# Feature-major projections of a two-layer sequence model: three 256-column products a step become one of 512 and one of 256

## The chip, the cores and the metric

One NeuronCore of a Trainium2 chip. The metric is device time in microseconds of one execution of the whole program, as the median of several runs. Five engines run side by side with their own instruction queues: TensorE (PE, with its weight loads shown as PEld), VectorE (DVE), ScalarE (ACT), GpSimd (POOL) and SyncE (SP, which issues most DMAs).

## The reference, cut to what matters

The model has 256 tokens, 1024 features and two layers. All data is float32.

```python
# layer 0
h = rms_norm(x, norm_w)
u = h @ w_in                      # 1024 -> 5408 columns
z_a, xbc, dt_raw, q_b, k_b, v_b, gate_lr, g_b = split_cols(u, EVEN_SPLITS)
xbc = silu(causal_depthwise_conv(xbc, conv_w, conv_b))
y_a = ssd_chunked_scan(xs, dt, a, bm, cm, d)        # state-space half
y_a = rms_norm(y_a * silu(z_a), ssd_norm_w)
o_b = gla_chunked(q_b, k_b, v_b, log_decay)         # gated linear attention half
o_b = rms_norm(o_b, gla_norm_w) * silu(g_b)
x = x + concatenate([y_a, o_b]) @ w_out
# layer 1
h = rms_norm(x, norm_w)
q, k, v, z = split_cols(h @ w_in, (1024, 1024, 1024, 1024))
o = moba_attention(q, k, v)       # 16 heads; here plain causal attention: one block of 256
x = x + (o * silu(z)) @ w_out
out = rms_norm(x, final_norm)
```

## The kernel before, in words

**Products in three parts.** Every large product is made from float32 operands cut in two: `hi`, the value rounded to the format that TensorE takes at its fast rate (float32r), and `lo`, the remainder. A product is then hi·hi + hi·lo + lo·hi, three matmuls that accumulate in one PSUM tile (`mm3`, lines 165 to 169). The contraction of 1024 is eight steps (`kb`) of 128 rows.

**Weights.** They come in pieces of up to 512 KB through the SyncE queue (`fetch`, line 70) and are split by `split` (line 75): ScalarE rounds `hi` (line 78), VectorE subtracts to get `lo` (line 79). Seven pieces are held split at a time (`NW`), and `need` (line 96) asks for a few pieces ahead of the one in use.

**Two forms of product.** In the *token-major* form (`gemm_tm`, `gemm_tt`, `part`) 128 tokens of activations are loaded as weights and 416 or 512 columns of the weight matrix stream past them. In the *feature-major* form (`gemm_fm`, line 290) 128 columns of the weight matrix are loaded and the 256 tokens of activations stream past, so the result has features on partitions. Feature-major are 26 blocks of the first projection (`pb`: blocks 0 to 9 are convolved, 10 to 13 are q and 14 to 17 k of the linear attention, 18 to 25 the gate z of the state-space half) and 24 of the attention layer's (`pp`: for each of 8 pairs of heads a q, a k and a z block). Each is 8 steps of 3 matmuls of 256 columns into the left half of a PSUM tile of 512; four such tiles rotate (`psg`).

**Evacuation.** A convolved block is scaled from PSUM into a padded buffer (`co_conv`, line 394), then four taps, a tanh and a product follow on ScalarE and VectorE. q and k blocks are copied from PSUM by ScalarE (line 578). A gate block is read from PSUM by VectorE (`gate_block`, line 591), then goes through tanh, products with `y` and a square for the norm (lines 593 to 601). In the attention layer q is copied in two halves by ScalarE (lines 748 and 749), of which only the second half is split in `hi` and `lo`; k is scaled by VectorE and split (752 to 754); z is scaled and gated (761 to 763).

**Order.** TensorE's order is fixed by the program. The projections are the main stream; the mixers (state-space pairs `co_pair`, linear attention `co_gla_pair`, attention `co_attn`) are generators whose steps are put between the projections' steps. Each `mm` adds its estimated TensorE time to a clock (`spend`, line 159), and a generator names the time that must pass before its next step (the table `DL`, line 28): `pair0` is the delay from a convolved block to its transposes, `cb` to the state-space score matrices, `gqk` before the linear attention's operands, `gla2` before the transposes `obt` of the linear attention's outputs `ob` (line 541), `at0` from a key block to the scores `as`, `at2` to the transposes `ptp` of the probabilities, `at3` to their product `ao` with the values. The other engines' queues are ordered by the compiler's scheduler, by data dependence, free buffers and the place in the program.

```python
def mm(out, lhsT, rhs, start=True, stop=True):
    ...
    TE.matmul(out, lhsT, rhs, start=start, stop=stop)
    spend(max(m / 1.2, n / 2.4) if lhsT.dtype == F32R else 2 * max(m / 1.2, n / 1.2))
```

Of the kernel before, what the change touches and what calls it, by code (L numbers as in the profile page):

```python
# [15 lines left out]
P = 128  # L16
# [6 lines left out]
NWARM = 20  # L23
# first weight pieces: (first row block, number of them)
CUTS_A0 = tuple((k, 1) for k in range(8))
AHEAD = 4
# tensor-engine time (ns) left to the other engines between the steps of a mixer
DL = {"ss": 1350, "rb": 5000, "gt": 1500, "ac": 7300, "act": 2600, "lg": 2150, "ln": 2250, "cb": 12400,
      "pair0": 11900, "pair1": 9700, "gla0": 650, "glagap": 3650, "gla1": 3350, "gla2": 8700, "r2": 10000,
      "turn": 4150, "rb1": 4000, "at0": 2600, "at2": 4350, "at3": 1800, "gqk": 250}  # L30
# feature-major blocks of the first projection: 0-9 convolved, 10-13 q, 14-17 k, 18-25 gate
# a1-a4: chunks of the token-major columns
ORDER_A = (8, 9, "a1", 0, 10, 1, 11, 2, 14, 3, 13, 5, 12, 4, 15, 16, 6, "a3", 7, 17, "a2", "a4")
GLA_NEEDS = ("a3", "a3", "a4", "a4")

# columns of the packed constants
C_EN, C_SN, C_ON = 0, 8, 16
C_CW, C_CB, C_GB, C_DS, C_GN = 24, 64, 74, 78, 86
C_DTB, C_AL = 87, 103
C_N = 119  # L40
# columns of the packed matrices of shape
M_ID, M_TRI, M_MASK, M_SEL = 0, 128, 384, 768
# [4 lines left out]
def trunk(ctx, tc, xT_d, x_d, cst_d, mat_d, gw2_d, fn_d, wa_d, wb_d, wc_d, wv_d, wp_d, wf_d, out_d):  # L47
# [20 lines left out]

    # ------------------------------------------------------------------ weights
    def fetch(src, kbs, cols, name):  # L70
# [53 lines left out]

    # ------------------------------------------------------------------ order of the tensor engine
    # The projections are the main stream; the mixers are generators that run beside it.
    # A generator yields the tensor-engine time (ns) after which its next step may be queued.
    clock = {"now": 0.0, "seq": 0}
# [16 lines left out]
    def due():  # L145
        while waiting and waiting[0][0] <= clock["now"]:
            step()
# [22 lines left out]

    # keep the tensor engine's clock up until the first operands arrive
    warm = cpool.tile([P, T], F32R, name="warm")
    V.memset(warm.bitcast(F32), 0.0)
# [3 lines left out]

    # ------------------------------------------------------------------ inputs
    xT = big.tile([P, KB, T], F32, name="xT", tag="xT")
    cst = cpool.tile([P, C_N], F32, name="cst")  # L180
    mat = cpool.tile([P, M_N], F32, name="mat")
    gw2 = cpool.tile([16, 512], F32, name="gw2")
    nc.scalar.dma_start(cst, cst_d)
# [19 lines left out]

    hhi = big.tile([P, KB, T], F32R, name="hhi", tag="hhi")
    hlo = big.tile([P, KB, T], F32R, name="hlo", tag="hlo")
    xsq = big.tile([P, KB, T], F32, name="xsq", tag="y")
# [43 lines left out]

    # ------------------------------------------------------------------ even in-projection
    v = big.tile([P, 2, D], F32, name="v", tag="v")
# [21 lines left out]
    def gemm_tm(name, hi8, lo8, cols, outs, cuts=((0, 2), (2, 2), (4, 2), (6, 2))):  # L274
        """Token-major product of both token tiles, a weight piece at a time."""
        for q_, (k0, n_) in enumerate(cuts):
            hi, lo = need((name, k0 if name == "a0" else q_))
            for tt in range(2):
                for j in range(n_):
                    kb = k0 + j  # L280
                    mm3(outs[tt][:, 0:cols], hi8[:, kb, tt * P:tt * P + P], lo8[:, kb, tt * P:tt * P + P],
                        hi[:, j, :], lo[:, j, :], kb == 0, kb == KB - 1)
# [6 lines left out]

    def gemm_fm(key, hi8, lo8, name):  # L290
        hi, lo = need(key)
        ps = pg(name)
        for kb in range(KB):
            mm3(ps[:, 0:T], hi[:, kb, :], lo[:, kb, :], hi8[:, kb, :], lo8[:, kb, :], kb == 0, kb == KB - 1)
        return ps[:, 0:T]

    def gemm_b(blk):
        return gemm_fm(("b", blk), hhi, hlo, f"pb{blk}")

# [17 lines left out]
    def co_first(ps):  # L317
# [11 lines left out]
        env["rb"] = True  # L329
        # softplus of the step sizes, by the series of artanh  # L330
        V.scalar_tensor_tensor(na, dtr, -1.0, dtr, op0=ALU.mult, op1=ALU.min)
# [29 lines left out]
        V.tensor_copy(acs, act[:, 0:32].rearrange("p (a b) -> p a b", a=2))  # L361
        # gate logits -> cumulated log decay (times 16)
        for b2 in range(2):
# [16 lines left out]

    # convolution and silu
    xs = big.tile([P, KB, T], F32, name="xs", tag="xT")
# [7 lines left out]
    def co_conv(blk, ps):  # L390
        while "rb" not in env:
            yield 100
        pd = pads[blk % 2]
        V.tensor_tensor(pd[:, 4:4 + T], ps, rb, op=ALU.mult)
        u = tmp.tile([P, T], F32, name=f"cu{blk}", tag="t1a")
        w = lambda i: cwh[:, 4 * blk + i:4 * blk + i + 1]
        S.activation(u, pd[:, 4:4 + T], AF.Identity, scale=w(3), bias=cwh[:, 40 + blk:41 + blk])
        for i in range(3):
            V.scalar_tensor_tensor(u, pd[:, 1 + i:1 + i + T], w(i), u, op0=ALU.mult, op1=ALU.add)
        th = tmp.tile([P, T], F32, name=f"cth{blk}", tag="t1b")  # L400
        S.activation(th, u, AF.Tanh)
        dst = xs[:, blk, :] if blk < 8 else bc[:, blk - 8, :]
        V.scalar_tensor_tensor(dst, th, 1.0, u, op0=ALU.add, op1=ALU.mult)
        if blk < 8:
            spawn(co_pair(blk))
        elif blk == 9:
            spawn(co_cb())
# [47 lines left out]

    # gated linear attention
    q = big.tile([P, 4, T], F32, name="q", tag="obhi")
# [108 lines left out]
    for blk in ORDER_A:  # L566
# [7 lines left out]
        if blk < 10:  # L574
            spawn(co_conv(blk, ps))
            due()
        else:
            S.activation((q if blk < 14 else k)[:, (blk - 10) % 4, :], ps, AF.Copy)
            env["nqk"] = env.get("nqk", 0) + 1
            if env["nqk"] == 8:  # L580
                spawn(co_gla_qk())

    # ------------------------------------------------------------------ gate of the state-space half
    x1 = big.tile([P, 2, D], F32, name="x1", tag="xT")
# [4 lines left out]
    def gate_block(b, ps):  # L589
        u = tmp.tile([P, T], F32, name=f"zu{b}", tag="t1a")  # L590
        V.scalar_tensor_tensor(u, ps, 0.5, rb, op0=ALU.mult, op1=ALU.mult)
        th = tmp.tile([P, T], F32, name=f"zth{b}", tag="t1b")
# [27 lines left out]

    # ------------------------------------------------------------------ even out-projection
    for n in range(2):
# [12 lines left out]
    def gemm_tt(name, hi8, lo8, tag):  # L635
        """Token-major product, one token tile after the other: yields each when it is done."""
        for tt in range(2):
            ps = pg(f"{tag}{tt}")
            part(ps, name, hi8, lo8, tt, range(KB), (name, 0) if tt == 0 else None)
            yield tt, ps  # L640

    ssn = sm.tile([P, 2, 2], F32, name="ssn", tag="ssn", bufs=1)
    h1hi = big.tile([P, KB, T], F32R, name="h1hi", tag="hhi")
    h1lo = big.tile([P, KB, T], F32R, name="h1lo", tag="hlo")

# [36 lines left out]

    # ------------------------------------------------------------------ second layer
    va = big.tile([P, 2, D], F32, name="va", tag="y")
# [54 lines left out]
    for pr in range(8):  # L739
        qk = []  # L740
        for i in range(2):
            ps = gemm_fm(("p", 3 * pr + i), h1hi, h1lo, f"pp{pr}_{i}")
            t_ = tmp.tile([P, T], F32, name=f"qk{pr}_{i}", tag=("t1a", "t1c")[i])
            n_ = (P, T)[i]
            hi = big.tile([P, n_], F32R, name=f"qkh{pr}_{i}", tag=(("cbT0", "cbT1"), ("qs", "ks"))[i][pr % 2])
            lo = big.tile([P, n_], F32R, name=f"qkl{pr}_{i}", tag=(("s3", "s4"), ("bc", "gs"))[i][pr % 2])
            if i == 0:
                S.activation(t_[:, 0:P], ps[:, 0:P], AF.Copy)
                S.activation(hi, ps[:, P:T], AF.Copy)
                V.tensor_sub(lo, ps[:, P:T], hi.bitcast(F32))  # L750
            else:
                V.tensor_tensor(t_, ps, rb1, op=ALU.mult)
                S.activation(hi, t_, AF.Copy)
                V.tensor_sub(lo, t_, hi.bitcast(F32))
            qk.append((t_, hi, lo))
        ops = pm(f"ao{pr}")
        spawn(co_attn(pr, *qk, ops))
        ps = gemm_fm(("p", 3 * pr + 2), h1hi, h1lo, f"pp{pr}_2")
        th = tmp.tile([P, T], F32, name=f"mth{pr}", tag="t1b")
        zs = tmp.tile([P, T], F32, name=f"zs{pr}", tag="t1e")  # L760
        V.scalar_tensor_tensor(zs, ps, 0.5, rb1, op0=ALU.mult, op1=ALU.mult)
        S.activation(th, zs, AF.Tanh)
        V.scalar_tensor_tensor(zs, th, 1.0, zs, op0=ALU.add, op1=ALU.mult)
        env[("z", pr)] = zs

    # ------------------------------------------------------------------ last projection and norm
    fnb = big.tile([P, D], F32, name="fnb", tag="s2")
# [124 lines left out]
```

## Time and profile before

| what | value |
|---|---|
| time, median of 3 runs | 349.83 us (348.47 to 350.31) |
| span of the profiled execution, first to last instruction | 347.5 us |
| its time as a run by itself | not among the three; the median stands 2.3 us above the span |
| TensorE / its weight loads, busy | 335.5 / 305.2 us |
| VectorE / ScalarE / GpSimd, busy | 263.5 / 217.5 / 49.3 us |
| matmuls | 2352, of them 1200 of the 256-column feature-major form |
| granted TensorE clock, mean | 0.995 of full speed |

Busy time is the union of an engine's instructions. Matmuls are pipelined: a product's record is longer than the distance to the next product's start, so the rate is read from starts, or from a long stretch of the chain of waits divided by its count. The chain of waits goes back from the last instruction, at each step to what released it, or to the instruction before it on its engine. In views by group, the first number behind the bar is the group's busy time in us, then the mean duration of one in ns, then the idle time of the engine just before them and what ended it. Names are the program's tile names without buffer numbers.

### The profile page before, as it was taken

The numbers are of one execution on the slowest core, as the hardware profiler recorded it, in microseconds if no ns is written. First come the engines' busy times: TensorE is split into PE (matmuls) and PEld (weight loads), VectorE is DVE, ScalarE is ACT, GpSimd is POOL, SyncE is SP. The second block draws the span as 40 slices with busy tenths as digits, with TensorE's granted clock in tenths as the row PEclk, the third lists the DMA queues.
The fourth block names the chain that finished last, engine by engine and source line by source line (L and its number), as shares of the span: only waits on it lengthen the run. The fifth ranks groups of instructions, "written<-read, shape, count | busy, mean of one in ns | idle before, by whom it ended". The sixth has DMA issues, their size and how long they took to land.

```text
span 347.5 us, 6341 instructions
## 1 busy us (share of the span) xinstructions
PE 335.5 (97%) x2352; PEld 305.2 (88%) x2352; DVE 263.5 (76%) x548; ACT 217.5 (63%) x445; POOL 49.3 (14%) x62
## 2 busy tenths in 40 slices
PE   8699999999999999999999999999999999999992
PEld 7599989998999899999888888899999999998792
DVE  5979999999989658789974775377777877777243
ACT  5547689898765757577542676466657665674222
POOL 2610001112415442434200000000000000000000
PEclk9999999999999999999999999999999999999998
DMA  7778672365573745631685634766344335430003
GB/s 209 238 245 283 219 255 94 80 185 178 162 227 115 252 132 170 186 117 41 207 296 189 201 121 163 241 210 214 124 158 146 123 122 183 122 123 0 3 0 121
DMA packets 17631, 56.09 MB, mean 161 GB/s; under 512 B 2096, under 2 KB 4144, under 8 KB 17472
## 3 DMA queue, kind: packets, MB, share of 16 engines
q1 hardware_dynamic: 16880, 53.53, 47.7%
q10 hardware_dynamic: 720, 2.16, 1.8%
q8 instruction: 18, 0.29, 0.4%
q14 instruction: 13, 0.11, 0.1%
HBM read 54.63 MB, written 1.05 MB: 160 GB/s over the span
## 4 chain that ended last, share of the span: by engine, by line
PE 85%; DVE 5%; issue 3%; DMA 2%; POOL 2%; SPq 0%; ACT 0%; POOLq 0%; DVEq 0%
PE pp L158 21%; PE pb L158 18%; PE pc L158 13%; PE pa L158 11%; PE pv L158 6%; PE pf L158 4%; DMA r_a<-in_wa 2%; PE ao L158 2%; PE yp L158 2%; PE as L158 2%; PE ptp L162 2%; PE gs L158 1%; PE go L158 1%; POOL rr L537 1%; POOL sT L517 1%
## 5 line engine op out<-in xcount | busy, mean ns | idle before, releaser
L158 PE MATMUL pb<-hhi,h_b 128*128 128x256 f32 x208 | 60.0, 288 | 0.0
L158 PE MATMUL pb<-hlo,h_b 128*128 128x256 f32 x208 | 58.7, 282 | 0.0
L158 PE MATMUL pb<-hhi,l_b 128*128 128x256 f32 x208 | 58.7, 282 | 0.0
L158 PE MATMUL pp<-h1hi,h_p 128*128 128x256 f32 x192 | 56.3, 293 | 0.0
L158 PE MATMUL pp<-h1lo,h_p 128*128 128x256 f32 x192 | 54.2, 282 | 0.0
L158 PE MATMUL pp<-h1hi,l_p 128*128 128x256 f32 x192 | 54.2, 282 | 0.0
L158 PEld LDWEIGHTS pb<-hhi,h_b 128*128 128x128 f32 x208 | 39.7, 191 | 1.2 <-issue 1.1
L158 PEld LDWEIGHTS pb<-hlo,h_b 128*128 128x128 f32 x208 | 39.7, 191 | 0.0
L158 PEld LDWEIGHTS pb<-hhi,l_b 128*128 128x128 f32 x208 | 39.7, 191 | 0.0
L79 DVE TENSOR_TENSOR l_p<-r_p,h_p 128x1024 fp32r<-128x1024 f32 x24 | 29.4, 1225 | 12.2 <-ACT h_p L78 11.6
L158 PEld LDWEIGHTS pp<-h1hi,h_p 128*128 128x128 f32 x192 | 36.6, 191 | 2.1 <-issue 1.0
L158 PEld LDWEIGHTS pp<-h1lo,h_p 128*128 128x128 f32 x192 | 36.6, 191 | 0.0
L158 PEld LDWEIGHTS pp<-h1hi,l_p 128*128 128x128 f32 x192 | 36.6, 191 | 0.0
L78 ACT ACTIVATE h_b<-r_b 128x1024 fp32r<-128x1024 f32 x26 | 27.4, 1067 | 9.5 <-DMA r_b<-in_wb 5.3
L79 DVE TENSOR_TENSOR l_b<-r_b,h_b 128x1024 fp32r<-128x1024 f32 x26 | 31.3, 1214 | 1.8 <-ACT h_b L78 1.8
L158 PE MATMUL pa<-l_a,hhi 128*128 128x416 f32 x80 | 28.4, 354 | 3.0 <-DVE l_a L79 3.0
L78 ACT ACTIVATE h_p<-r_p 128x1024 fp32r<-128x1024 f32 x24 | 25.3, 1056 | 9.5 <-PE pp L158 5.4
L158 PE MATMUL pa<-h_a,hhi 128*128 128x416 f32 x80 | 29.0, 363 | 0.1
L158 PE MATMUL pa<-h_a,hlo 128*128 128x416 f32 x80 | 28.2, 353 | 1.0 <-DVE hlo L215 1.0
L79 DVE TENSOR_TENSOR l_a<-r_a,h_a 128x832 fp32r<-128x832 f32 (+1 forms) x24 | 22.8, 960 | 2.2 <-ACT h_a L78 2.2
L79 DVE TENSOR_TENSOR l_c<-r_c,h_c 128x1024 fp32r<-128x1024 f32 x16 | 19.9, 1252 | 4.8 <-ACT h_c L78 4.8
L78 ACT ACTIVATE h_c<-r_c 128x1024 fp32r<-128x1024 f32 x16 | 16.9, 1056 | 10.1 <-DMA r_c<-in_wc 6.3
(241 smaller groups left out, 804.4 us busy)
## 6 DMA issues: line engine op xcount, KB each, us to landing
r_b<-in_wb SPq DMA_DIRECT2D x26, 512.0 KB, 4.2
r_p<-in_wp SPq DMA_DIRECT2D x24, 512.0 KB, 4.0
r_c<-in_wc SPq DMA_DIRECT2D x16, 512.0 KB, 4.2
r_a<-in_wa SPq DMA_DIRECT2D x16, 416.0 KB, 3.6
r_v<-in_wv SPq DMA_DIRECT2D x8, 512.0 KB, 4.5
r_f<-in_wf SPq DMA_DIRECT2D x8, 512.0 KB, 3.5
r_a<-in_wa SPq DMA_DIRECT2D x8, 208.0 KB, 3.6
xT<-in_xT SPq DMA_DIRECT2D x8, 128.0 KB, 3.6
```

The lines of the kernel that those rows point to most:

```text
L78: S.activation(hi, raw, AF.Copy)
L79: V.tensor_sub(lo, raw, hi.bitcast(F32))
L158: TE.matmul(out, lhsT, rhs, start=start, stop=stop)
L162: TE.transpose(out, in_, ident)
L517: G.affine_select(out=sT[:, 0:3:2, :], in_=sT[:, 0:3:2, :], pattern=[[0, 2], [1, P]], compare_op=ALU.is_ge, fill=0.0, base=0, channel_mult ...
L537: G.tensor_tensor(rr, ss, mhalf, op=ALU.pow)
```

## The change

Feature-major products take the activations' high and low parts side by side. The two tiles `hhi` and `hlo` become one tile `hh` with both for each step, and so do `h1hi` and `h1lo`. A step multiplies the high weights by both parts at once, 512 columns into the whole PSUM tile, and the low weights by the high part, 256 columns into the left half. The halves are added behind the product by the new helper `joined`: ScalarE copies the right half to SBUF, VectorE adds it to the left half. All 50 blocks are evacuated through it, and the scaling that used to read PSUM follows in place. Four delays of the planner are longer (`cb`, `pair0`, `at0` by 900, `gqk` by 450). The warm-up tile and the gate's second weight matrix move into shared buffers.

```diff
-DL = {... "cb": 12400, "pair0": 11900, ... "at0": 2600, ... "gqk": 250}
+DL = {... "cb": 13300, "pair0": 12800, ... "at0": 3500, ... "gqk": 700}
...
-    warm = cpool.tile([P, T], F32R, name="warm")
+    warm = big.tile([P, T], F32R, name="warm", tag="s0")
...
-    gw2 = cpool.tile([16, 512], F32, name="gw2")
+    gw2 = big.tile([16, 512], F32, name="gw2", tag="s4")
...
-    hhi = big.tile([P, KB, T], F32R, name="hhi", tag="hhi")
-    hlo = big.tile([P, KB, T], F32R, name="hlo", tag="hlo")
+    hh = big.tile([P, KB, 2, T], F32R, name="hh", tag="hh")
+    hhi, hlo = hh[:, :, 0, :], hh[:, :, 1, :]
...
-    def gemm_fm(key, hi8, lo8, name):
+    def gemm_fm(key, act, name):
         hi, lo = need(key)
         ps = pg(name)
         for kb in range(KB):
-            mm3(ps[:, 0:T], hi[:, kb, :], lo[:, kb, :], hi8[:, kb, :], lo8[:, kb, :], kb == 0, kb == KB - 1)
-        return ps[:, 0:T]
+            if kb < KB - 1:
+                mm(ps, hi[:, kb, :], act[:, kb, :, :], kb == 0, False)
+            mm(ps[:, 0:T], lo[:, kb, :], act[:, kb, 0, :], False, False)
+            if kb == KB - 1:
+                mm(ps, hi[:, kb, :], act[:, kb, :, :], False, True)
+            due()
+        return ps
+
+    def joined(out, ps, name):
+        second = tmp.tile([P, T], F32, name="jn" + name, tag="t1h")
+        S.activation(second, ps[:, T:2 * T], AF.Copy)
+        V.tensor_tensor(out, ps[:, 0:T], second, op=ALU.add)
...
-        V.tensor_tensor(pd[:, 4:4 + T], ps, rb, op=ALU.mult)
+        joined(pd[:, 4:4 + T], ps, f"c{blk}")
+        V.tensor_tensor(pd[:, 4:4 + T], pd[:, 4:4 + T], rb, op=ALU.mult)
...
-            S.activation((q if blk < 14 else k)[:, (blk - 10) % 4, :], ps, AF.Copy)
+            joined((q if blk < 14 else k)[:, (blk - 10) % 4, :], ps, f"qk{blk}")
...
-        V.scalar_tensor_tensor(u, ps, 0.5, rb, op0=ALU.mult, op1=ALU.mult)
+        joined(u, ps, f"z{b}")
+        V.scalar_tensor_tensor(u, u, 0.5, rb, op0=ALU.mult, op1=ALU.mult)
...
-            if i == 0:
-                S.activation(t_[:, 0:P], ps[:, 0:P], AF.Copy)
-                S.activation(hi, ps[:, P:T], AF.Copy)
-                V.tensor_sub(lo, ps[:, P:T], hi.bitcast(F32))
-            else:
-                V.tensor_tensor(t_, ps, rb1, op=ALU.mult)
-                S.activation(hi, t_, AF.Copy)
-                V.tensor_sub(lo, t_, hi.bitcast(F32))
+            joined(t_, ps, f"p{pr}_{i}")
+            if i == 1:
+                V.tensor_tensor(t_, t_, rb1, op=ALU.mult)
+            S.activation(hi, t_[:, T - n_:T], AF.Copy)
+            V.tensor_sub(lo, t_[:, T - n_:T], hi.bitcast(F32))
...
-        V.scalar_tensor_tensor(zs, ps, 0.5, rb1, op0=ALU.mult, op1=ALU.mult)
+        joined(zs, ps, f"g{pr}")
+        V.scalar_tensor_tensor(zs, zs, 0.5, rb1, op0=ALU.mult, op1=ALU.mult)
```

## Rows read from the trace of the kernel before

**Rows 1.** The page, part 1: busy time, share of the span and instructions.
```profile
PE 335.5 (97%) x2352; PEld 305.2 (88%) x2352; DVE 263.5 (76%) x548; ACT 217.5 (63%) x445; POOL 49.3 (14%) x62
```

**Rows 2.** The chain of waits in order of time: start us, length us, what.
```profile
53.80 8.62 PE pb L158 x72
...
64.66 0.80 PE yp L158 x8
...
212.09 17.04 PE pv L158 x75
229.12 9.35 PE pp L158 x78
```

**Rows 3.** TensorE's waits, all of them: total us, times, longest.
```profile
PE pa L158 <- DVE l_a L79: 3.0, 3, 2.0
PE warmp L176 <- DVE mhalf L199: 1.3, 1, 1.3
PE pa L158 <- DVE hlo L215: 1.0, 1, 1.0
```

**Rows 4.** Busy time by stretch: length; PE, PEld, DVE, ACT, POOL; clock, DMA, GB/s.
```profile
26.00:54.00 28.00, 28.00 (x196) 26.16 (x196) 26.83 (x56) 22.53 (x35) 0.00 (x0) 1.00 0.75 251
54.00:104.00 50.00, 50.00 (x393) 47.02 (x392) 45.96 (x71) 41.36 (x78) 10.15 (x14) 1.00 0.50 152
104.00:131.00 27.00, 27.00 (x189) 24.66 (x188) 19.76 (x43) 16.00 (x41) 12.55 (x13) 1.00 0.50 167
131.00:162.00 31.00, 30.92 (x274) 29.88 (x273) 26.75 (x69) 23.12 (x57) 10.10 (x14) 1.00 0.41 130
...
229.00:317.00 88.00, 88.00 (x756) 82.87 (x755) 67.32 (x180) 54.72 (x135) 0.00 (x0) 1.00 0.46 149
26.00:162.00 136.00, 135.92 (x1044) 127.73 (x1044) 119.30 (x236) 103.02 (x208) 32.81 (x40) 1.00 0.53 170
```

**Rows 5.** Groups by line and shape: evacuations and an SBUF operation of 256 columns.
```profile
L394 DVE TENSOR_TENSOR pad<-pb,rb 128x256 f32<-128x256 f32 x10 | 4.2, 417 | 0.0
...
L754 DVE TENSOR_TENSOR qkl<-qk,qkh 128x256 fp32r<-128x256 f32 x8 | 3.3, 418 | 0.0
...
L578 ACT ACTIVATE k<-pb 128x256 f32<-128x256 f32 x4 | 1.6, 389 | 0.0
```

**Rows 6.** VectorE in order of time, in the gate stretch: start us, length us, what.
```profile
147.13 0.42 DVE L591 SCALAR_TENSOR_TENSOR zu<-pb,rb 128x256 f32<-128x256 f32 x1
...
154.26 0.42 DVE L591 SCALAR_TENSOR_TENSOR zu<-pb,rb 128x256 f32<-128x256 f32 x1
154.60 1.12 DVE L541 SCALAR_TENSOR_TENSOR ob<-go,rr,gs 128x128 f32<-128x128 f32 x4
...
157.09 0.41 DVE L591 SCALAR_TENSOR_TENSOR zu<-pb,rb 128x256 f32<-128x256 f32 x1
157.42 2.15 DVE L612 SCALAR_TENSOR_TENSOR ylo<-y,cst,yhi 128x256 fp32r<-128x256 f32 x4
```

**Rows 7.** GpSimd and TensorE's weight loads there, in order of time.
```profile
149.90 1.45 POOL L537 TENSOR_TENSOR rr<-oss,mhalf 128x2 f32<-128x2 f32 x2 [2.88 <-DVE oss L536]
...
155.77 0.20 PEld L162 LDWEIGHTS obt<-mat,ob 128*128 128x128 f32 x2 [0.31 <-DVE ob L541]
```

**Rows 8.** The attention layer in order of time: ScalarE, VectorE, TensorE around one key block.
```profile
267.29 1.06 ACT L78 ACTIVATE h_p<-r_p 128x1024 fp32r<-128x1024 f32 x1 [0.70 <-PE pp L158]
...
269.53 0.42 DVE L754 TENSOR_TENSOR qkl<-qk,qkh 128x256 fp32r<-128x256 f32 x1
...
270.44 0.38 PE L158 MATMUL as<-qk,qk 64*128 64x128 f32 x2
```

**Rows 9.** VectorE and TensorE in order of time, 61 to 72 us.
```profile
61.38 0.95 DVE L444 TENSOR_TENSOR e<-e,cbT 128x768 f32<-128x768 f32 x1
...
63.37 1.21 DVE L79 TENSOR_TENSOR l_b<-r_b,h_b 128x1024 fp32r<-128x1024 f32 x1
...
71.56 0.28 PE L158 MATMUL pb<-hhi,l_b 128*128 128x256 f32 x1
```

More of the change, by code (lines that the diff above doesn't have):

```diff
@@ L26 @@
 AHEAD = 4
-DL = {"ss": 1350, "rb": 5000, "gt": 1500, "ac": 7300, "act": 2600, "lg": 2150, "ln": 2250, "cb": 12400,
-      "pair0": 11900, "pair1": 9700, "gla0": 650, "glagap": 3650, "gla1": 3350, "gla2": 8700, "r2": 10000,
-      "turn": 4150, "rb1": 4000, "at0": 2600, "at2": 4350, "at3": 1800, "gqk": 250}
+DL = {"ss": 1350, "rb": 5000, "gt": 1500, "ac": 7300, "act": 2600, "lg": 2150, "ln": 2250, "cb": 13300,
+      "pair0": 12800, "pair1": 9700, "gla0": 650, "glagap": 3650, "gla1": 3350, "gla2": 8700, "r2": 10000,
+      "turn": 4150, "rb1": 4000, "at0": 3500, "at2": 4350, "at3": 1800, "gqk": 700}
 ORDER_A = (8, 9, "a1", 0, 10, 1, 11, 2, 14, 3, 13, 5, 12, 4, 15, 16, 6, "a3", 7, 17, "a2", "a4")
@@ L293, in gemm_fm @@
         for kb in range(KB):
-            mm3(ps[:, 0:T], hi[:, kb, :], lo[:, kb, :], hi8[:, kb, :], lo8[:, kb, :], kb == 0, kb == KB - 1)
-        return ps[:, 0:T]
+            if kb < KB - 1:
[9 more added lines that the diff above has]
+        V.tensor_tensor(out, ps[:, 0:T], second, op=ALU.add)
     def gemm_b(blk):
-        return gemm_fm(("b", blk), hhi, hlo, f"pb{blk}")
+        return gemm_fm(("b", blk), hh, f"pb{blk}")
     def st(name):
@@ L642, in trunk @@
     ssn = sm.tile([P, 2, 2], F32, name="ssn", tag="ssn", bufs=1)
-    h1hi = big.tile([P, KB, T], F32R, name="h1hi", tag="hhi")
-    h1lo = big.tile([P, KB, T], F32R, name="h1lo", tag="hlo")
+    h1 = big.tile([P, KB, 2, T], F32R, name="h1", tag="hh")
+    h1hi, h1lo = h1[:, :, 0, :], h1[:, :, 1, :]
     def co_turn(tt, n):
@@ L741, in trunk @@
         for i in range(2):
-            ps = gemm_fm(("p", 3 * pr + i), h1hi, h1lo, f"pp{pr}_{i}")
+            ps = gemm_fm(("p", 3 * pr + i), h1, f"pp{pr}_{i}")
             t_ = tmp.tile([P, T], F32, name=f"qk{pr}_{i}", tag=("t1a", "t1c")[i])
@@ L757, in trunk @@
         spawn(co_attn(pr, *qk, ops))
-        ps = gemm_fm(("p", 3 * pr + 2), h1hi, h1lo, f"pp{pr}_2")
+        ps = gemm_fm(("p", 3 * pr + 2), h1, f"pp{pr}_2")
         th = tmp.tile([P, T], F32, name=f"mth{pr}", tag="t1b")
         zs = tmp.tile([P, T], F32, name=f"zs{pr}", tag="t1e")
-        V.scalar_tensor_tensor(zs, ps, 0.5, rb1, op0=ALU.mult, op1=ALU.mult)
+        joined(zs, ps, f"g{pr}")
+        V.scalar_tensor_tensor(zs, zs, 0.5, rb1, op0=ALU.mult, op1=ALU.mult)
         S.activation(th, zs, AF.Tanh)
```

## The prediction

> **What bounds the kernel now.** I read the page first: TensorE is busy for 335.5 of 347.5 us, 97% [rows 1]. A busy TensorE can still be one that waits inside, so next come its own waits: three entries, 5.3 us in all, every one of the opening, where the first activations and weights are still being split [rows 3]. After that its products follow each other almost without a gap (it is busy in 135.92 of the 136 us from 26 to 162 [rows 4]), and the chain of waits accordingly consists of stretches of its products [rows 2]. So the time is the number of products times their spacing, and the spacing is what I read from the chain: 72 products of 256 columns in 8.62 us and 78 in 9.35 us are 119.7 and 119.9 ns each; 75 products of 512 columns in 17.04 us are 227.2 ns each [rows 2]. Twice the columns cost 1.90 times the time: about 12.4 ns of a product do not grow with its columns.
>
> Last I read how near the others are to taking over. VectorE is busy 26.83 of 28 us and 45.96 of 50 us in the stretches from 26 to 104 us, where the convolution runs; 26.75 of 31 us from 131 to 162 us, where the gate of the state-space half runs; and 67.32 of 88 us in the attention layer. ScalarE stays below it in each [rows 4].
>
> **The change, part by part.** *Products.* Each of 50 feature-major blocks (26 of the first projection, 24 of the attention layer) has 8 steps of three 256-column products; a step becomes one of 512 and one of 256. Before: 3 x 119.8 = 359.4 ns. After: 227.2 + 119.8 = 347.0 ns. 12.4 ns x 400 steps = 5.0 us less, 2.6 us of it in the first layer and 2.4 us in the second. This lies wholly on the path. The planner's clock charges a step the same as before (213 + 107 ns for three times 107), so apart from the four changed delays the order on TensorE stays.
>
> The alternation 512, 256, 512 is in no row. The rows on either side of it are the two uniform streams; I take their sum, with a gain of 5.3 us at the good end (the spread of spacings in steady stretches is about 1 ns) and no gain at the other, if changing the width eats the 12.4 ns. By the Trainium skill (TensorE: Matmul & The Clock Gate, Back-to-back issue gap) a warm product takes columns/2.4 plus 2.5 ns; by that a step would save only 2.5 ns, 1.0 us in all, and the sum below would end at +1.1 us instead of -2.9. This trace does not agree: its spacings stand 13 to 14 ns above columns/2.4.
>
> *The halves.* Each block gains a ScalarE copy of 128x256 out of PSUM and a VectorE addition of 128x256. The nearest rows are the copy of k, 389 ns, and the scaling into the convolution's pad, 417 ns [rows 5]. Back to back VectorE starts the next such operation 0.33 us later (157.09 to 157.42) [rows 6]. So 50 additions are 16.5 to 20.9 us more on VectorE. On ScalarE 34 copies are new (10 convolution, 8 gate, 16 k and z of the attention); the 8 of q and k in the first layer exist already, and 8 for the attention's q replace two copies of half the size by one full and one half. The multiplications that used to read PSUM now read SBUF in place; I price that at nothing: one operation of that size from PSUM takes 417 ns, one from SBUF 418 [rows 5].
>
> None of this is on TensorE, so its price is what it makes late. The copy waits for the block's last product; queued behind it on ScalarE are weight roundings and exponentials. The addition waits for the copy; behind it on VectorE are weight splits and the mixers' operations. Weights have room: between 45 and 160 us the tightest split I found ends at 64.58 us for a product at 71.56 us [rows 9], 7.0 us ahead (earlier ones stand closer, but only the first blocks' additions come before 45 us). Decay matrices have less: e is ready at 62.33 us [rows 9] for products at 64.66 us [rows 2], 2.3 us. From 26 to 104 us VectorE has 5.2 us idle [rows 4] and gets 17 additions, 5.6 us at 0.33: it fills up, and about a microsecond of backlog goes into those 2.3 and 7.0 us. The longer delays before the pair and before the attention cover the longer evacuation itself. I put 0.4 us of stalls here; bounds 0 and the 7.1 us that 17 x 0.417 would be with no cover at all.
>
> *The gate stretch* has no such cover. There the transposes of the linear attention's outputs already wait 0.31 us for VectorE's ob [rows 7]. POOL's rr, on which ob depends, is done at 151.35 us [rows 7], yet ob starts at 154.60: VectorE takes other work first, and from 147.13 to 154.26 three gate blocks' first operations [rows 6] and weight splits pass before ob. Each of these three blocks now brings an addition ahead of its first operation: 3 x 0.33 = 1.0 us later. The delay gla2 stays at 8700 ns, 27 steps of 320 on the planner's clock, so TensorE comes to the transposes 27 x 12.4 ns = 0.3 us earlier. So 1.3 us of new stall; bounds 0 (VectorE is given ob ahead of the gates) and 3.3 us (all 8 gate additions at 0.417 land in front).
>
> *The attention layer.* A key block ends just before 267.29 us, when ScalarE's next weight rounding is released; the key's low half, on VectorE, ends at 269.95 us, and the scores start at 270.44 us [rows 8]: 0.5 us of room. Evacuation grows by a copy and an addition, 0.39 + 0.33 = 0.7 us, and I allow 0.1 us for the two hand-overs. The delay at0 moves the scores from 6 steps after the key block to 8; at 347 ns a step that is 0.6 us later. Room left: 0.3 us. The copy can also go ahead of that weight rounding and so hide part of itself. From the scores to the next transposes (at2, 4350 ns, 14 steps) 0.17 us of room goes too. I take 0.05 us for each of 8 pairs, 0.4 us; bounds 0 and 8 x 0.8 = 6.4 us if none is covered.
>
> *At nothing:* the merged activation tile (same writes, same bytes), the warm-up tile and the gate's weights in shared buffers (free again before their next tenants are written), no DMA moved or added.
>
> **Sum.** -5.0 + 0.4 + 1.3 + 0.4 = -2.9 us. The profiled execution spans 347.5 us; the runs' median of 349.83 us is 2.3 us above it, and I carry the difference over: **346.9 us**.
>
> **Rivals.** *A, the forecast:* most of the saving stays, 346 to 348.5 us.
>
> *B, VectorE becomes the bound; slower.* Place: 26 to 162 us, with 119.3 us of VectorE work in 136 [rows 4]. With 26 additions at 0.417 it is 130.1 us, against 136 - 2.6 = 133.4 us of TensorE. That fits only if VectorE gives up most of its 16.7 us idle, and some of that is forced, since it waits in order for POOL and ScalarE. It decides when 8.3 us of idle stay: 130.1 + 8.3 = 138.4 us, 2.4 us longer than now, which cancels the second layer's gain. With all 16.7 kept: 146.8 us, 10.8 longer, 358.2 us in the end; with three quarters, 354.1 us. For it: the stretch to 104 us is at 93%. Against: 7.2 us of idle from 104 to 131 us, where few blocks come, and splits that run 7 us and more ahead.
>
> *C, everything is hidden:* VectorE's order shifts around ob and TensorE never waits: 344.8 us. For it: splits done far ahead can be put off for nothing.
>
> *D, the change does not shorten the products:* what I read as 12.4 ns per product is lost again in the alternation. Gain 0 to 2 us against 2.1 us of stalls: 349.9 to 351.9 us. The Trainium skill's formula, above, is near this case. Against it: three streams of two widths agree with a constant part.
>
> **Chances.** A 0.45, B 0.22, C 0.20, D 0.13. A measurement here tells from no change about 0.5%, 1.75 us. A gives 0.37 faster and 0.08 within; C 0.20 faster; D 0.07 within and 0.06 slower; B 0.04 within and 0.18 slower. Together 0.57, 0.19, 0.24. Range: down to 344.0 us (C, with 5.3 us and the runs' spread), up to 352.0 us (D whole and B's lower part); 0.03 and 0.15 are left out. A and C alone: 344.0 to 348.5 us.
>
> **What would show it.** Right: 400 fewer products, 512-column ones in pb and pp about 227 ns before the next start and 256-column ones about 120; VectorE 16 to 21 us busier; TensorE's list of waits with a new entry for ob in the gate stretch of 1 to 2 us and small ones in the attention. Wrong in the products: steps of 359 ns. Wrong in the cover: TensorE waits on l_b, e or qkl by several us, or VectorE without idle time up to 162 us. Wrong in the gate term: no wait on ob at all.

## The result and the profile after

The changed kernel is slower by about 1%: 352.98 us, median of 10 runs (350.67 to 355.64), against 349.88 us of the kernel before in 10 runs on the same chip (348.35 to 351.14). The ratio is 1.0105 [1.0081, 1.0128]. The forecast of 346.9 us had the wrong sign, and the time lies above its range.

The profiled execution of the changed kernel took 354.5 us and spans 352.6 us, 5.1 us more than the span before. Of the ten runs the four with a mean granted clock of 0.985, this one among them, took 353.18 to 355.64 us and the three at 0.994 to 0.996 took 350.67 to 352.23 us, so the profile shows a larger loss than the medians do (3.1 us). Its page, part 1 [rows 1]:

```profile
PE 337.6 (96%) x1952; PEld 286.1 (81%) x1952; DVE 278.9 (79%) x598; ACT 230.6 (65%) x479; POOL 46.4 (13%) x62
```

The 400 products are gone (2352 to 1952), and VectorE is 15.4 us busier with 50 more operations, just under the 16.5 to 20.9 us forecast. So the change does what it says. TensorE's own waits in the changed kernel [rows 3]:

```profile
PE pa L158 <- DVE l_a L79: 2.7, 2, 1.9
PE obt L162 <- DVE ob L555: 1.7, 1, 1.7
PE warmp L176 <- DVE mhalf L199: 1.3, 1, 1.3
PE pa L158 <- DVE hh L215: 1.0, 1, 1.0
PE go L158 <- DVE sT L533: 0.9, 2, 0.5
PE gs L158 <- ACT e L452: 0.4, 1, 0.4
PE yp L158 <- DVE ob L555: 0.3, 1, 0.3
```

Before, there were three entries, all of the opening. Now there are four more after 100 us. The one of 1.7 us on ob was forecast, in its place; those on sT, e and ob at yp were not, and the entry for l_a holds 0.9 us at 115 us. The stretches of the changed kernel show where [rows 4]:

```profile
26.00:54.00 28.00, 28.00 (x157) 24.14 (x156) 25.20 (x56) 22.57 (x37) 0.00 (x0) 1.00 0.67 210
54.00:104.00 50.00, 49.87 (x305) 42.18 (x304) 46.15 (x80) 40.95 (x82) 9.95 (x14) 1.00 0.51 147
104.00:131.00 27.00, 24.61 (x167) 21.55 (x166) 24.24 (x41) 17.92 (x39) 8.52 (x11) 1.00 0.58 187
131.00:168.00 37.00, 35.22 (x227) 30.50 (x226) 30.67 (x86) 27.08 (x71) 12.67 (x17) 0.95 0.40 130
101.03:133.73 32.70, 30.31 (x198) 26.84 (x197) 28.87 (x54) 20.79 (x47) 11.37 (x14) 1.00 0.61 189
```

From 26 to 104 us VectorE was given 16 additions (the forecast counted 17), and yet it is busy for 25.20 + 46.15 = 71.4 us, where it was 26.83 + 45.96 = 72.8 before. It did not fill up. The additions pushed other work out of this stretch, and that work comes after 104 us: 24.24 us busy in 27, where it was 19.76. There TensorE stands still for 2.4 us (24.61 of 27). Before, it was busy all the time.

The last row is one stretch by its ends, from the block at 101.03 us to the next block at 133.73 us. The kernel before has the same two blocks at 101.45 and 130.53 us:

```profile
101.45:130.53 29.08, 29.08 (x206) 26.75 (x205) 21.16 (x44) 18.29 (x45) 12.64 (x13) 1.00 0.53 177
```

So here 3.6 us of the 5.1 are lost (32.70 against 29.08), in a stretch that the prediction counted as one with room. The first block at 101 us comes even 0.4 us earlier than before.

One piece of the work that was pushed out, in VectorE's order of time, in the changed kernel:

```profile
102.22 1.22 DVE L486 TENSOR_TENSOR e<-gcs 128x1024 f32<-128x1024 f32 x1
```

The same subtraction, operand of the linear attention, ran at 58.34 us before:

```profile
58.34 1.22 DVE L472 TENSOR_TENSOR e<-gcs 128x1024 f32<-128x1024 f32 x1
```

What that does to TensorE shows in one weight split, that of TensorE's wait for l_a at 115 us: its rounding on ScalarE, then the split itself on VectorE, in the changed kernel:

```profile
98.99 0.90 ACT L78 ACTIVATE h_a<-r_a 128x832 fp32r<-128x832 f32 x1 [0.56 <-DMA r_a<-in_wa]
```

```profile
114.22 1.95 DVE L79 TENSOR_TENSOR l_a<-r_a,h_a 128x832 fp32r<-128x832 f32 x2
```

The same split in the kernel before:

```profile
100.18 1.02 DVE L79 TENSOR_TENSOR l_a<-r_a,h_a 128x832 fp32r<-128x832 f32 x1
```

The two halves of the line at 114.22 us are two splits; the first is meant. Before, it ended at 101.20 us for a product at 115.08 us, 13.9 us ahead. In the changed kernel its input is ready at 99.89 us, but VectorE, busy from 101 to 119 us without a wait of 0.1 us, reaches it at 114.22 us, and TensorE waits 0.9 us for it.

The other loss is at the gate stretch. TensorE in order of time, changed kernel (in brackets the idle time before and what ended it):

```profile
158.11 0.28 PE L158 MATMUL pb<-hh,l_b 128*128 128x256 f32 x1
160.09 0.95 PE L162 MATMUL obt<-mat,ob 128*128 128x128 f32 x4 [1.70 <-DVE ob L555]
...
161.34 0.63 PE L158 MATMUL pb<-hh,h_b 128*128 128x512 f32 x1
161.78 0.41 PE L158 MATMUL pb<-hh,l_b 128*128 128x256 f32 x1
161.99 0.63 PE L158 MATMUL pb<-hh,h_b 128*128 128x512 f32 x1
...
164.87 0.40 PE L158 MATMUL pb<-hh,h_b 128*128 128x512 f32 x1
```

After the 1.70 us of idle time the 512-column products start 0.44 us before the next, then 0.21 us pass after a 256-column one: half speed. The windows of the same kernel show it as the granted clock, before, in and after it:

```profile
159.00:160.00 1.00, 0.00 (x0) 0.00 (x0) 1.00 (x5) 0.79 (x3) 0.23 (x1) 1.00 0.62 139
161.00:164.80 3.80, 3.80 (x15) 3.24 (x14) 3.80 (x11) 3.30 (x9) 0.73 (x1) 0.55 0.06 24
165.00:166.00 1.00, 1.00 (x8) 0.86 (x7) 1.00 (x4) 1.00 (x2) 0.00 (x0) 1.00 0.00 0
```

TensorE was idle for 1.70 us, and then for 3.8 us it was granted 0.55 of its clock, the 1.2 GHz level for most of it: 3.8 x 0.45 = 1.7 us of its work lost. With the 1.7 us of the wait, the block at 164.53 us is 6.3 us late (158.20 before), where the one ahead of it, at 157.53 us, was 2.9 us late: 3.4 us lost here.

The attention layer, with the products of its output, gave back 1.2 us: it starts 6.3 us late, and its last product ends 5.1 us late.

### The profile page after: what moved, and what is told of

Same layout as the page of the kernel before. It is cut to its first block, busy times and chain, and to the rows that moved or that the text cites. A ratio compares the mean times of both kernels' runs of the same rounds, so it can differ in the third digit from the quotient of the medians.

```text
span 352.6 us, 5576 instructions
## 1 busy us (share of the span) xinstructions
PE 337.6 (96%) x1952; PEld 286.1 (81%) x1952; DVE 278.9 (79%) x598; ACT 230.6 (65%) x479; POOL 46.4 (13%) x62
## 4 chain that ended last, share of the span: by engine, by line
PE 62%; DVE 15%; issue 10%; POOL 4%; ACT 4%; DMA 4%; POOLq 0%; SPq 0%; DVEq 0%; ACTq 0%
PE pp L158 20%; PE pc L158 12%; PE pb L158 9%; PE pv L158 6%; PE pf L158 4%; PE pa L158 2%; DVE l_b L79 2%; DMA r_a<-in_wa 2%; DMA r_b<-in_wb 2%; PE ao L158 2%; PE as L158 2%; PE ptp L162 1%; POOL e L456 1%; DVE l_a L79 1%; PE yp L158 1%
## 5 line engine op out<-in xcount | busy, mean ns | idle before, releaser
L158 PE MATMUL pb<-hh,h_b 128*128 128x512 f32 x208 | 75.7, 408 | 0.0
L158 PE MATMUL pp<-h,h_p 128*128 128x512 f32 x192 | 69.4, 407 | 0.0
L158 PE MATMUL pb<-hh,l_b 128*128 128x256 f32 x208 | 55.5, 285 | 0.0
L158 PE MATMUL pp<-h,l_p 128*128 128x256 f32 x192 | 50.0, 281 | 0.0
L158 PE MATMUL pa<-h_a,hh 128*128 128x416 f32 x160 | 47.7, 367 | 1.0 <-DVE hh L215 1.0
L158 PEld LDWEIGHTS pb<-hh,h_b 128*128 128x128 f32 x208 | 38.9, 193 | 7.6 <-issue 0.8
L158 PEld LDWEIGHTS pb<-hh,l_b 128*128 128x128 f32 x208 | 40.2, 193 | 2.2 <-issue 0.2
L158 PEld LDWEIGHTS pp<-h,h_p 128*128 128x128 f32 x192 | 34.9, 188 | 7.9 <-issue 1.0
L158 PEld LDWEIGHTS pp<-h,l_p 128*128 128x128 f32 x192 | 36.2, 189 | 1.9
L158 PEld LDWEIGHTS pa<-h_a,hh 128*128 128x128 f32 x160 | 31.1, 195 | 2.4 <-DVE hh L215 1.2
```

## The experiments

The runs decide between two readings of the loss. *Amount*: VectorE can't take the additions in the first layer, so the loss follows their time, wherever it shows. *Order*: an addition moves one critical piece (ob, or the linear attention's operands) behind other work, so putting that piece right recovers the loss. Beside them stands the size of the products' saving. Each ratio is to the kernel before on the same chip.

**products_only.** The wide products stay; every block is evacuated as before, from the left half, with the old delays. It leaves out the product of the high weights with the low activations.

```diff
-        joined(pd[:, 4:4 + T], ps, f"c{blk}")
-        V.tensor_tensor(pd[:, 4:4 + T], pd[:, 4:4 + T], rb, op=ALU.mult)
+        V.tensor_tensor(pd[:, 4:4 + T], ps[:, 0:T], rb, op=ALU.mult)
```

> The wide products of the change, but every block evacuated as before from the left half alone; delays as before, storage as changed. Left out: the product of high weights and low activations in the feature-major blocks. Theory 'cover' (the saving in products is there, the additions cost more than it): 400 steps at the 352 ns that the changed kernel shows instead of 359.4, 3.0 us below the kernel before, about 346.9 us, and no wait of TensorE on ob or l_a after 25 us. Theory 'alternation' (the change of width eats the whole saving): 349.9 us. Theory 'storage' (the tiles moved into shared buffers displace the linear attention's operands): 352 us or more, with these operands made at about 102 us as in the changed kernel.

Measured: 346.35 us, 0.9923 [0.9898, 0.9947], 3.0 us under the 349.35 us before, and no wait of TensorE after the opening. The products save 3.0 us, not 5.0. By the profiled spans it is 2.2 us; there this kernel's third block, at 36.69 us, is already 0.6 us late from the opening.

**joins_only.** The products as before, with the copy and the addition. The copy reads the left half times zero, so nothing is left out of the sum.

```diff
+            mm3(ps[:, 0:T], hi[:, kb, :], lo[:, kb, :], act[:, kb, 0, :], act[:, kb, 1, :], kb == 0, kb == KB - 1)
...
-        S.activation(second, ps[:, T:2 * T], AF.Copy)
+        S.activation(second, ps[:, 0:T], AF.Copy, scale=0.0)
```

> The additions without the wide products: three products of 256 columns a step as before, and every block evacuated as in the changed kernel, the copied half scaled by zero and read from the left half. Delays and storage as changed. 'Cover': slower than the changed kernel by the products' saving, some 355 to 356 us. 'Alternation': the products make no difference, so the same as the changed kernel, 353 us.

Measured: 357.45 us, 1.0244 [1.0211, 1.0278], 8.1 us more than the 349.35 us before, and more than either expectation. The evacuation alone costs more than twice what the products save. The spans almost add up: 345.3 - 347.5 = -2.2 us here and 355.3 - 347.5 = +7.8 us make +5.6, against +5.1 measured with both.

**gla2_later.** Only the delay before the transposes of ob changes.

```diff
-DL = {... "gla2": 8700 ...}
+DL = {... "gla2": 10700 ...}
```

> The changed kernel with the delay gla2 10700 instead of 8700. 'Cover': the last transposes obt come six steps later, their 2.0 us wait on ob goes, and with it the 3.6 us stretch at half the granted clock behind it; 1.5 to 3.4 us less than the changed kernel, 349.6 to 351.5 us. Rival 'backlog' (VectorE is late as a whole, so the wait moves to the next consumer): 353 us, with another wait of 2 us or more between 155 and 175 us.

Measured: 351.37 us, 1.0069 [1.0034, 1.0105]. TensorE waits for ob 0.3 us instead of 1.7, and the stretch at the lower clock behind it is gone. So the wait at the gate is a matter of order, and can be had back: 1.6 us by the medians (the interval overlaps that of the changed kernel, so it is the trace that shows it). The rest stays.

**early_operands.** The subtractions and exponentials of the linear attention get high priority, so that they run where they ran before. **early_and_gla2** joins the two edits.

```diff
-        V.tensor_tensor(e2, gcs, gcs[:, :, 32:33].to_broadcast(full), op=ALU.subtract)
...
+        with tc.high_priority():
+            V.tensor_tensor(e2, gcs, gcs[:, :, 32:33].to_broadcast(full), op=ALU.subtract)
...
```

> The changed kernel, with the two subtractions and four exponentials that prepare the linear attention's operands from gcs marked as high priority, so that they are made right behind the scan at about 60 us, as in the kernel before, instead of at 102 to 107 us. Nothing else. Theory 'order' (the additions fill VectorE's queue, the scheduler puts these operands off to where they meet the state-space pairs, the weight splits and the scores, and there TensorE waits): the 3.6 us that the changed kernel loses between 101 and 134 us go, 349.4 us. Rival 'amount' (VectorE has too much to do from 26 to 131 us in any order): 353 us, with the waits somewhere else before 134 us.

> The early operands and gla2 10700 together. 'Order': both losses of the changed kernel, 3.6 us and 2 to 3.4 us, go; 346.5 to 348 us, faster than the kernel before. 'Amount': 351 us or more.

Measured: 354.6 us, 1.014 [1.011, 1.0169], and 353.2 us, 1.0096 [1.0065, 1.0127]. The operands are early again (the first subtraction starts at 61.66 us in early_operands), and nothing is gained. TensorE still waits for ob, and now also earlier, as three entries of its list in early_operands show:

```profile
PE obt L162 <- DVE ob L556: 1.6, 1, 1.6
PE xtp L162 <- DVE xs L417: 1.5, 2, 1.1
PE acp L158 <- DVE dta L356: 0.7, 1, 0.7
```

The wait for dta and the longer one for xs fall before 67 us: a block that starts at 64.14 us before, and at 64.23 in the changed kernel, starts at 66.90 (1.1 us of that is there from the opening). Between the block of 101 us and that of 134 us early_operands loses 1.9 us instead of 3.6, but it comes there 2.9 us late. Moving these operands up moved the lateness and did not remove it. This speaks for *amount*, against *order*.

**old_delays.** The changed kernel with the four delays of before.

```diff
-DL = {... "cb": 13300, "pair0": 12800, ... "at0": 3500, ... "gqk": 700}
+DL = {... "cb": 12400, "pair0": 11900, ... "at0": 2600, ... "gqk": 250}
```

> The changed kernel with the four delays cb, pair0, at0 and gqk as in the kernel before. If the longer delays do what they are there for, TensorE now waits on xs for the transposes and on qkl for the scores (8 times about 0.3 us each and more): 354 to 357 us. Theory 'delays' (the longer delays moved the mixers into a worse place): 350 to 351 us.

Measured: 351.94 us, 1.0066 [1.0037, 1.0094]. Neither expectation came true. Without the longer delays TensorE does wait for xs, but the kernel is no slower than with them. Its interval overlaps that of the changed kernel, so whether the longer delays cost the 1.0 us between the medians isn't decided; most of the loss is not theirs. It only moves: the block of 64.14 us starts at 67.12 us after a wait of 2.4 us for xs, and the one of 130.53 us (133.73 in the changed kernel) starts at 133.84. It is the same 3.3 us late, lost before 67 us instead of after 101.

**copies_only** and **adds_only** take the evacuation apart. The first issues the ScalarE copy of the right half, unused, and evacuates as before. The second adds a constant tile of zeros on VectorE, without copy or hand-over. Both leave out the product of the high weights with the low activations.

```diff
-        V.tensor_tensor(out, ps[:, 0:T], second, op=ALU.add)
```

```diff
-        S.activation(second, ps[:, T:2 * T], AF.Copy)
-        V.tensor_tensor(out, ps[:, 0:T], second, op=ALU.add)
+        V.tensor_tensor(out, ps[:, 0:T], zero, op=ALU.add)
```

> The changed kernel with ScalarE's copies of the right halves but without VectorE's additions; the left half is evacuated as before. Left out: the product of high weights and low activations in the feature-major blocks. Theory 'VectorE' (the additions' time on VectorE, on top of about 10 us in which it waits for others between 36 and 131 us whatever it is given, sets the length of that stretch): near the products-only kernel, 346.3 to 347.5 us. Rival 'ScalarE' (the copies delay the exponentials and weight roundings): 350 us or more.

> The changed kernel with VectorE's additions but without ScalarE's copies: a constant tile of zeros is added. Left out: the product of high weights and low activations in the feature-major blocks. 'VectorE': near the changed kernel, 351.5 to 353 us. 'ScalarE': 346.5 to 347.5 us. If it is the hand-over between the two that costs, both this and the copies-only kernel come out at 346.5 to 348 us.

Measured: copies_only 347.33 us, 0.9949 [0.993, 0.9968]; adds_only 352.63 us, 1.0109 [1.0079, 1.0138]. The additions alone give the whole loss. copies_only stands 1.0 us above products_only by the medians, but the intervals overlap and it has the longer delays too, so a cost of the copies isn't shown. adds_only also makes the way from product to operand one operation longer. For the wait for l_a this is no rival, since a weight split stands behind no evacuation (the lines above); for the waits on sT, e and ob VectorE's time and the longer way aren't told apart. One window a kernel shows how VectorE takes it, each from the third block of the first projection to its nineteenth (the two that stand at 36.06 and 130.53 us before): length, then busy times as in [rows 4], here the kernel before, the changed one, products_only, joins_only and adds_only in turn.

```profile
36.06:130.53 94.47, 94.47 (x711) 87.58 (x710) 82.45 (x140) 71.39 (x138) 22.62 (x26) 1.00 0.55 173
```

```profile
36.25:133.73 97.48, 94.96 (x583) 80.67 (x582) 87.55 (x159) 73.58 (x147) 19.53 (x26) 1.00 0.56 167
```

```profile
36.69:130.16 93.47, 93.47 (x583) 80.25 (x582) 82.47 (x140) 71.55 (x139) 24.70 (x26) 1.00 0.53 175
```

```profile
35.73:135.96 100.23, 96.88 (x711) 89.30 (x710) 89.01 (x162) 74.30 (x149) 20.15 (x26) 0.98 0.50 163
```

```profile
35.98:134.50 98.52, 95.92 (x583) 82.12 (x582) 88.37 (x157) 70.00 (x133) 17.85 (x26) 0.98 0.53 166
```

VectorE's idle time, length less its busy time, is 12.0, 9.9, 11.0, 11.2 and 10.2 us. (The windows of joins_only and adds_only hold 3.4 us at the 1.2 GHz level, 0.98 in the mean, which is 1.7 us of their length.) VectorE's busy time grows by 5.1 to 6.6 us with the additions, and its idle time hardly shrinks, though TensorE now waits for it. Part of what ended its waits from 26 to 131 us in the changed kernel (total us, times, longest):

```profile
DVE e L458 <- POOL e L456: 3.3, 6, 0.7
DVE xs L417 <- ACT cth L415: 1.8, 1, 1.8
DVE cu L413 <- ACT cu L411: 1.1, 1, 1.1
```

These are 6.2 of the 9.4 us that it is idle there (105 less 25.20 + 46.15 + 24.24). The kernel before has the first of them too, in the same stretch:

```profile
DVE e L444 <- POOL e L442: 3.6, 6, 0.7
```

The additions left that wait much as it was (3.6 and 3.3 us). VectorE takes its operations in the order of its queue, and while it waits for GpSimd's e it doesn't take a split that is ready behind:

```profile
98.08 0.96 DVE L458 TENSOR_TENSOR e<-e,cbT 128x768 f32<-128x768 f32 x1 [0.66 <-POOL e L456]
...
99.35 1.02 DVE L79 TENSOR_TENSOR l_a<-r_a,h_a 128x832 fp32r<-128x832 f32 x1
```

The input of this split was rounded by 95.61 us. That such waits are the reason why VectorE didn't fill up is read from the traces; no run takes them away.

**adds_on_pool.** In the first layer's convolution, q, k and gate blocks ScalarE copies both halves and GpSimd adds them.

```diff
+            S.activation(out, ps[:, 0:T], AF.Copy)
+            G.tensor_tensor(out, out, second, op=ALU.add)
```

> The changed kernel, but in the first layer ScalarE copies both halves and GpSimd, idle there for most of the time, adds them; VectorE's 26 additions of that layer go. 'VectorE': the stretch before 131 us shortens by the work taken off, up to 3.6 us, and the total falls to 349 to 351 us, unless GpSimd's own waits delay the causal masks, which the trace would show as TensorE or VectorE waiting for GpSimd. Rival 'latency' (it is the longer way from product to operand that costs): slower than the changed kernel, 354 us or more.

Measured: 357.81 us, 1.0243 [1.0212, 1.0275], worse than on VectorE. The forecast of 'VectorE' failed, and the time lies where the rival 'latency' put it. Three groups of its page, GpSimd's additions and two of VectorE's operations:

```profile
L310 POOL TENSOR_TENSOR pad<-pad,jnc 128x256 f32<-128x256 f32 x10 | 11.0, 1096 | 21.6 <-ACT pad L309 21.6
L417 DVE SCALAR_TENSOR_TENSOR cu<-pad,cwh,cu 128x256 f32<-128x256 f32 x30 | 16.5, 551 | 0.1
L462 DVE TENSOR_TENSOR e<-e,cbT 128x768 f32<-128x768 f32 x8 | 10.6, 1330 | 4.6 <-POOL e L460 4.6
```

The same two in the changed kernel:

```profile
L413 DVE SCALAR_TENSOR_TENSOR cu<-pad,cwh,cu 128x256 f32<-128x256 f32 x30 | 14.5, 482 | 1.1 <-ACT cu L411 1.1
L458 DVE TENSOR_TENSOR e<-e,cbT 128x768 f32<-128x768 f32 x8 | 7.8, 978 | 3.3 <-POOL e L456 3.3
```

An addition takes GpSimd 1.10 us (VectorE 0.42), and VectorE's own operations grow from 482 to 551 and from 978 to 1330 ns. So VectorE gains nothing (it is busy for 96.75 us from 26 to 131 us, 95.59 in the changed kernel), and the added chain is longer: TensorE waits 2.0 us for xs, 2.4 for y and 2.7 for ob. Both changed at once, so this run doesn't tell amount from latency.

**second_layer** keeps the change for the attention layer alone, with the first layer's products, evacuation and delays as before (`wide` is true for the blocks of the attention layer). **second_grouped** changes only the order in its blocks: seven wide products, the eight narrow ones, the last wide one.

```diff
+            if not wide:
+                mm3(ps[:, 0:T], hi[:, kb, :], lo[:, kb, :], act[:, kb, 0, :], act[:, kb, 1, :], kb == 0, kb == KB - 1)
+                continue
```

```diff
         for kb in range(KB):
...
             if kb < KB - 1:
                 mm(ps, hi[:, kb, :], act[:, kb, :, :], kb == 0, False)
+                due()
+        for kb in range(KB):
             mm(ps[:, 0:T], lo[:, kb, :], act[:, kb, 0, :], False, False)
-            if kb == KB - 1:
-                mm(ps, hi[:, kb, :], act[:, kb, :, :], False, True)
             due()
+        mm(ps, hi[:, KB - 1, :], act[:, KB - 1, :, :], False, True)
+        due()
```

> Wide products and additions only in the attention layer's 24 blocks; the first layer's 26 as before, with its old delays. 'Cover': in the changed kernel the attention layer took 1.2 us less than before while all the loss lay before 168 us, so 1.2 us below the kernel before, 348.7 us. 'Alternation': 349.9 us. 'Storage': 352 us.

> Wide products and additions only in the attention layer, and in each of its blocks seven 512-column products first, then the eight 256-column ones, then the last 512-column one: two changes of width a block instead of sixteen. Theory 'alternation costs': a step falls from 352 to 347 ns, 192 x 5 ns = 1.0 us less than the same kernel with alternating products, 347.3 us, with 227 ns between the wide starts. Rival (the width of the product before does not matter, a wide product of a new weight costs 233 ns in these blocks): 348.2 us and 233 ns.

Measured: 348.25 us, 0.9963 [0.9939, 0.9986], and 347.22 us, 0.9946 [0.9923, 0.9968]. In the attention layer, where VectorE has room, the change pays. Grouping pays as well, by the profile: the chain of waits gives the time from one pair of heads to the next, 24 steps, by the starts of two equal stretches. In turn the kernel before, the changed one, products_only, second_grouped:

```profile
271.29 5.22 PE pp L158 x42
...
282.50 5.22 PE pp L158 x42
```

```profile
266.51 5.14 PE pp L158 x28
...
277.60 5.14 PE pp L158 x28
```

```profile
269.88 5.10 PE pp L158 x28
...
280.91 5.10 PE pp L158 x28
```

```profile
270.45 4.95 PE pp L158 x26
...
281.45 4.95 PE pp L158 x26
```

They are 11.21, 11.09, 11.03 and 11.00 us. With the short delay `at0` (products_only) the alternation saves 0.18 us a pair, 7.5 ns a step. In the changed kernel, with the long one, it saves 0.12 us. The additions don't make this difference: old_delays, with additions and the short delay, repeats after 11.03 us, and copies_only, with the long delay and no additions, after 11.08. It goes with `at0`, which decides between which products the attention's steps stand. Grouped, with the long delay, a pair saves 0.21 us, 9 ns a step, of the 12.4 that were forecast.

From the layer's first product to the end of the output's last, second_layer takes 107.87 us and second_grouped 107.33. So grouping is worth 0.5 us over the layer. The intervals of the two overlap, and of the 1.5 us between their profiled spans 0.9 lie in the opening, so the traces show this gain and the times alone don't. second_grouped leaves nothing out and has the lowest median of the versions that don't: its interval lies below that of the changed kernel and below 1.

## Why the prediction was wrong

*The bound* was read rightly: TensorE sets the end, and the time follows its spacing and its waits.

*Products, -5.0 us: mis-sized.* They gave 3.0 us (median) or 2.2 us (span). The step was taken as the sum of two uniform streams, 347.0 ns. In the alternation a 512-column product is followed after 233 to 235 ns (227 alone) and a 256-column one after 117 ns (119.8 alone), in the median. Away from the mixers' steps a step takes 350 ns (median; 341 to 361). The prediction named this as the unknown and had bounds of 0 and 5.3 us around it, but took the value at one end. Grouped, the wide products come back only in part: of 153 that are followed by another wide one, 66 are followed after 224 to 229 ns, and the median is 231. The Trainium skill's formula (TensorE: Matmul & The Clock Gate, Back-to-back issue gap), which the prediction weighed, lets a step save 2.5 ns (the page calls it the gap of an isolated product); taken off the 359.4 ns measured before, that is an estimate of 356.9 ns, and the trace stands between it and the forecast.

*The cover from 26 to 104 us, 0.4 us: the step that failed.* "It fills up" was the assumption, with about a microsecond of backlog. VectorE didn't fill up: it was busy for 71.4 us there, 72.8 before, so other work as long as the 16 additions, 16 x 0.417 = 6.7 us, went behind the stretch. Its idle time is forced in part, in order, by GpSimd and ScalarE (read from its waits, not tested). Against products_only, block by block, 3.8 us are lost between 101 and 134 us, 3.3 us at the gate and 0.2 us in the attention layer. That is 7.3 us with what lies between, where 2.1 us were forecast, and 345.3 + 7.3 is the span of 352.6 us. The prediction looked for the lateness inside the stretch that gets the additions. It came behind it, from 115 us on, because work without an early due time was put off (the subtractions at 102 us, the split at 114 us) until it was due. The 7.2 us of idle from 104 to 131 us, held against rival B, had to take this backlog: 2.8 us of it are left, and TensorE waited all the same.

*Rival B* named the mechanism, "some of that is forced", with 8.3 us of idle as the point from which it decides. The idle time left was about 10 us from 36 to 134 us alone. B got 0.22 and should have stood first: how much of an engine's idle time is forced can be read from what ended its waits, and the forecast did not read it.

*The gate, 1.3 us: right wait, wrong price.* The wait is 1.7 us for ob, in its place, and gate additions stand ahead of ob as forecast. In the changed kernel, GpSimd's rr, the last addition before ob, and ob:

```profile
153.57 1.34 POOL L551 TENSOR_TENSOR rr<-oss,mhalf 128x2 f32<-128x2 f32 x2 [3.39 <-DVE oss L550]
...
159.10 0.42 DVE L308 TENSOR_TENSOR zu<-pb,jnz 128x256 f32<-128x256 f32 x1
159.43 1.12 DVE L555 SCALAR_TENSOR_TENSOR ob<-go,rr,gs 128x128 f32<-128x128 f32 x4
```

From rr to ob pass 4.52 us, where it was 3.25 (151.35 to 154.60). Not foreseen was the clock behind the wait, about 1.7 us more.

*The attention layer, 0.4 us:* it cost 0.2 us against products_only, and no wait of TensorE stands there. The size is about right, the reason only in part: with the short `at0` the additions cost 0.2 us (107.90 us for the layer in old_delays, 107.66 in products_only). With the long one they cost nothing, but the delay itself costs as much (107.88 in the changed kernel, 107.87 in copies_only, which has no additions).

*Rival D* explains 2 us of the miss, by its mechanism, but not the loss. *At nothing:* the shared buffers are not the cause, since second_layer keeps them and has the operands' subtraction back at 58.62 us.

Open is the opening: from 17.5 to 21.1 us the granted clock is 0.53 in the changed kernel, 0.57 in products_only and 0.56 in second_layer, and 1.00 in the kernel before, joins_only and second_grouped. By the third block the changed kernel is 0.2 us behind the kernel before, products_only 0.6 and second_layer 0.3 us, and second_grouped is 0.6 us ahead. What makes the clock fall there wasn't tried.

## What to carry to other kernels

Idle time of an engine that runs in order is a reserve only as far as nothing forces it: list what ended its waits before giving it work, and look for the lateness where the put-off work falls due, not where the new work sits. Where a change trades a few nanoseconds of a saturated engine for a third of a microsecond on a nearly full one, make it only in the stretches with room (here the attention layer). Products of different widths are worth issuing in runs of one width; here it gave 0.5 us over 24 blocks.

## What was unexpected in the hardware

In the changed kernel an idle gap of 1.7 us on TensorE was followed by 3.8 us at a granted clock of 0.55, so that the wait cost twice its length. Without the gap (gla2_later) the clock stayed at 1.00 there. Not every such gap does this: after one of 2.36 us in old_delays (for xs, at 65 us) and one of 1.61 us in early_operands (for ob, at 162 us) it stayed at 1.00 as well.

VectorE's operations on SBUF grew while GpSimd worked on SBUF beside it: with GpSimd's additions, the 22 of the convolution's multiply-adds that met no GpSimd instruction took at most 487 ns, and the eight that met one took 764 ns in the mean and 959 at the longest. The Trainium skill says why (SBUF — State Buffer, Who interferes with whom): a VectorE instruction with two SBUF inputs and a GpSimd instruction that reads SBUF contend for a shared port pair, which it calls "an exclusive lock". The trace agrees, with single operations held up by half a microsecond; it does not show the port itself.
